# Conv columns scaled once by the squared row factor, the heads' forms on one engine, and a staging tile with a second use

## The chip, the cores and the metric

The kernel runs on one core of one Trainium2 chip. The metric is the device time of one launch in microseconds (us); less is better. A core has a matrix engine (TensorE, PE in the profile, with its weight loads as PEld), three engines for elementwise work (VectorE or DVE, ScalarE or ACT, GpSimd or POOL), a queue that issues transfers (SP) and 16 DMA engines. The engines run on their own and wait for each other by semaphores. Operands lie in on-chip memory (SBUF); TensorE writes its sums to PSUM banks.

## The reference

One layer of a hybrid encoder is applied to 512 prompt frames and 64 sample frames (576 together) of width 2048, in fp32. What matters here is the middle of it:

```
hn = rmsnorm(x, g_norm1);  proj = hn @ w_in
q, k, v, gb, gc, hc = split(proj)          # 8 heads x 128, and three times 1024 conv channels
u = gc * hc
conv = conv_w[0]*u[t-2] + conv_w[1]*u[t-1] + conv_w[2]*u[t]
o_conv = gb * conv
mix = concat(rmsnorm(o_attn, g_attn_out), rmsnorm(o_conv, g_conv_out))
x = x + mix @ w_out                         # then a gated feed-forward block, untouched by the change
```

`rmsnorm(y, g) = y * rsqrt(mean(y*y) + EPS) * g`, with EPS = 1e-6. The first norm multiplies each frame (row) by a factor R = rsqrt(mean(x*x) + EPS). It is not applied to x ahead of the product but to what comes out of it: q, k and v per head, and the three conv columns gb, gc and hc. The last two rows of u are an output (the conv state), so u itself has to come out with its true scale.

## The kernel before

**Layout.** Frames lie along the free dimension, channels on the 128 partitions. The 576 frames are worked in two halves of 288 (`HALVES`). Every fp32 operand of a product is held as two parts, a high part rounded to the matrix format and the low rest: `split` makes the high part with a ScalarE copy (L230) and the low part with a VectorE subtraction (L231), or on another engine where one is given. A product of two such operands is three matmuls of 128x288.

**Stages.** First the eight heads, each with three column chunks of w_in (`head`, `project`). Then the conv channels: the first two of eight groups in the plain way (`conv_group`, `STD = 2`), the other six in nine *units* of two groups' columns each. A unit is computed by a scheme with 7 half-size products for 8 (`conv_run`), whose operands are sums of quarters of the weights and of the frames. Units are of kind u (gc and hc of one group, six of them) and b (gb of two groups, three of them). Products are numbered here as they stand in `corder`: product 0 is (unit 0, part 1), then (0,2), (1,1), (1,2), (0,7), (0,6), (0,5), (0,3), (0,4), (1,6), (1,7), (1,5), (2,1), (1,3), (1,4). Then eight units "o" multiply the heads' outputs by w_out in the same way, and `out_proj` multiplies the conv outputs. The feed-forward block follows.

**The row factor in the conv columns.** `R1` holds R, the same on all partitions, 128x576. In the plain groups the gate gc is multiplied by R1 twice on its way out of PSUM (L960, L961), since gc and hc each want one factor, hc is multiplied by the gate straight from PSUM (`put_u`, L933 and L935), and gb is multiplied by R1 (L975) before the taps (L950, L952). In the units `done` multiplies each of the four quarters by R1 (L1112), after the addition of a partial sum where there is one (L1110). `put_mix` makes the two parts of the result times g_conv_out, stores them to DRAM and adds their squares to `acc_c` (squares on ScalarE, the addition on POOL at L538). Late in the o units, `group_scale` splits those sums, adds them over the channels with a product against ones (`channel_sums`) and turns them into the factor `R_c` (`rsqrt_mean`).

**The heads' forms.** Once the heads are done, `head_forms` normalises their outputs and makes, for each of four pairs of heads, the seven *forms* (three quarters and four differences of quarters) that the o units need. Each form is split into the staging tile `bt["stage"]` (named hf in the profile; eight slots of two parts, used in turn) and stored to DRAM (L580). The sums of squares of the heads, `acc_a`, are split ahead of that into two tiles of the pool tag hl (two buffers, which `put_mix` uses as well). The four differences per pair are made on POOL (L586), the low parts of forms 5 and 6 on POOL too, all else on VectorE.

**What sets the order.** The work beside the products is written as generators that a small scheduler (`Pipeline`) advances by one tick per step of a product, so it is spread in the program between the matmuls. TensorE's order is the program's. ScalarE, VectorE, POOL and SP are ordered by a planner that simulates the program with modelled durations, except in stretches set by hand; from the last half of the second conv group to product 8, ScalarE and VectorE go in program order (`start_mode`). `conv_prepare` makes the operands of a product (`whl`) some products ahead, `begin` sets which at the start, and `call_columns` loads the next weight columns as soon as a half of `raw_a`, or `raw_c`, is free. All form stores, weight loads and the loads of frame sums (xs) are issued on SP, in order.

Of the kernel before, what the change touches and what calls it, by code (L numbers as in the profile page):

```python
# [13 lines left out]
ALU = mybir.AluOpType  # L14
PSUM = bass.MemoryType.PSUM

P = 128
TP = 512
TS = 64
T = TP + TS  # L20
HALF = T // 2
HALVES = ((0, HALF), (HALF, T))
# [9 lines left out]
EPS = 1e-6  # L32
NEG = -1.0e30
QB = TP // P
NP = KD // 2
# [59 lines left out]
def tile_hybrid_stream_step(  # L95
# [6 lines left out]
    nc = tc.nc  # L102
# [20 lines left out]
    NB = T // 32  # L123
    eps_r, gk_t, quad = small[:, :NB], small[:, NB : NB + 32], small[:, NB + 32 : NB + 36]
# [39 lines left out]
    def weight_raw(i):  # L164
        src, nk, ncol = specs[i]
        raw = raw_tile["A"][:, i % 2, : nk * ncol]
        return raw, raw.rearrange("p (k c) -> p k c", k=nk), src
# [61 lines left out]
    def split(hi, lo, src, lo_eng=None):  # L229
        nc.scalar.copy(out=hi, in_=src)  # L230
        (lo_eng or nc.vector).tensor_tensor(out=lo, in0=src, in1=hi.bitcast(F32), op=ALU.subtract)  # L231

    def parts(name):
        t = tmp.tile([P, 2, HALF], F32R, tag="hl", name=name)
        return t[:, 0], t[:, 1]
# [72 lines left out]
    def col(name, i=0):  # L308
        return vec[:, rows[name] + i : rows[name] + i + 1]
# [18 lines left out]
    R1 = rpool.tile([P, T], F32, tag="R", name="R1", bufs=2)  # L328
# [63 lines left out]
    with tc.manual_schedule(engines={mybir.EngineType.Activation, mybir.EngineType.DVE, mybir.EngineType.SP}):  # L392
        raw, raw3, src = weight_raw(0)
# [25 lines left out]
        for kt in range(KD + LAG):  # L419
# [21 lines left out]
            if kt == 16:  # L441
                nc.vector.tensor_tensor(out=lo1[:, :1024], in0=raws[1][:, :1024], in1=hi1[:, :1024].bitcast(F32),  # L442
                                        op=ALU.subtract)
# [7 lines left out]
        while squares:  # L451
# [13 lines left out]
                            in1=quad.unsqueeze(1).to_broadcast([P, 5, 4]), op=ALU.mult)  # L465
# [17 lines left out]

    hpool.release()

    def rsqrt_mean(dst, src, n, width, ms=None, t=None):
        if ms is None:
            ms = tmp.tile([P, HALF], F32, tag="ms", name="ms", bufs=1)[:, :width]
            t = tmp.tile([P, HALF], F32, tag="t", name="t", bufs=1)[:, :width]
        y = tmp.tile([P, HALF], F32, tag="y", name="y")[:, :width]  # L490
        nc.vector.tensor_scalar(out=ms, in0=src, scalar1=1.0 / n, scalar2=EPS, op0=ALU.mult, op1=ALU.add)
        nc.scalar.activation(out=y, in_=ms, func=AF.Ln)
        nc.scalar.activation(out=y, in_=y, func=AF.Exp, scale=-0.5)
        nc.vector.tensor_tensor(out=t, in0=y, in1=y, op=ALU.mult)
        nc.vector.scalar_tensor_tensor(out=t, in0=t, scalar=-0.5, in1=ms, op0=ALU.mult, op1=ALU.mult)
        nc.vector.scalar_tensor_tensor(out=dst, in0=t, scalar=1.5, in1=y, op0=ALU.add, op1=ALU.mult)
# [58 lines left out]
    def head_forms():  # L555

        turn = [0]
        two = [parts("sqg") for _ in HALVES]  # L560
        for (sh, sl), (a, b) in zip(two, HALVES):
            split(sh, sl, acc_a[:, a:b])
        yield 6
        for (sh, sl), (a, b) in zip(two, HALVES):
            rsqrt_mean(acc_a[:, a:b], channel_sums(sh, sl, a, b, "ssg"), 8 * P, HALF)
            yield 4
        for k in range(NH // 2):
            pair = o_half[k // 2][:, 2 * (k % 2) : 2 * (k % 2) + 2, :]
            four = pair.rearrange("p k (i t) -> p (k i) t", i=2)
            b11, b12, b21, b22 = (four[:, q, :] for q in range(4))  # L570
            for r in range(2):
                nc.vector.scalar_tensor_tensor(out=pair[:, r], in0=pair[:, r], scalar=col("ga", 2 * k + r), in1=acc_a,
                                               op0=ALU.mult, op1=ALU.mult)
            yield 2

            def put(f, src, lo_eng):
                t = bt["stage"][:, turn[0] % NP]
                turn[0] += 1
                split(t[:, 0], t[:, 1], src, lo_eng)
                nc.sync.dma_start(out=form_dram[f - 1, k].rearrange("f p t -> p f t"), in_=t.bitcast(F32))  # L580

            for f, src in ((1, b11), (2, b21), (3, b22)):
                put(f, src, nc.vector)
                yield 2
            for f, out, a, b in ((5, b11, b12, b11), (7, b12, b12, b22), (6, b22, b22, b11), (4, b21, b21, b22)):
                nc.gpsimd.tensor_tensor(out=out, in0=a, in1=b, op=ALU.subtract)  # L586
                yield 1
                put(f, out, nc.gpsimd if f in (5, 6) else nc.vector)
                yield 2
            if k == 1:  # L590
                bt["raw"] = apool.tile([P, 2048], F32, tag="oa", name="raw_c")
                assert cwanted[0] == (1, 0)
                call_columns([2])

    def group_scale(acc, dst, rows_of):

        four = cpool.tile([P, 2, 2, HALF], F32R, tag="uc", name="sqg")
        for i, (a, b) in enumerate(HALVES):
            sh, sl = four[:, i, 0], four[:, i, 1]
            split(sh, sl, acc[:, a:b])  # L600
            yield rows_of
            ss = channel_sums(sh, sl, a, b, "ssg")
            ms, t = (tmp.tile([P, HALF], F32, tag=tag, name=tag + "g") for tag in ("r", "sq"))
            rsqrt_mean(dst[:, a:b], ss, 8 * P, HALF, ms, t)
            yield rows_of

    acc_a = rpool.tile([P, T], F32, tag="R", name="acc_a", bufs=2)
# [289 lines left out]
    bt = {}  # L897
# [45 lines left out]
            nc.vector.scalar_tensor_tensor(out=c, in0=u[:, r : UW - 2 + r], scalar=col("cw", r * NG + g), in1=c,  # L943
                                           op0=ALU.mult, op1=ALU.add)

    def put_o(g, i, t):

        a, b = HALVES[i]
        c, e = taps(g), min(b, TP)
        nc.vector.tensor_tensor(out=t[:, : e - a], in0=t[:, : e - a], in1=c[:, a:e], op=ALU.mult)  # L950
        if b > TP:
            nc.vector.tensor_tensor(out=t[:, e - a :], in0=t[:, e - a :], in1=c[:, TP + 2 :], op=ALU.mult)  # L952
        put_mix(g, i, t, col("gc", g), bt["acc"][:, a:b], g == 0)

    def conv_group(g):
        gates = []

        def evac_gc(ps, a, b):
            t = tmp.tile([P, HALF], F32, tag="sq", name="gcr")
            nc.vector.tensor_tensor(out=t, in0=ps, in1=R1[:, a:b], op=ALU.mult)  # L960
            nc.vector.tensor_tensor(out=t, in0=t, in1=R1[:, a:b], op=ALU.mult)  # L961
            gates.append(t)

        project(evac_gc)
        begin_u(g)
        project(lambda ps, a, b: put_u(a, b, ps, gates[a // HALF]),
                then=(lambda: call_columns(range(2))) if g == STD - 1 else None)

        def evac_gb(ps, a, b):
            if not bt:  # L970
                open_b()
            if a == 0:
                end_u(g)
            t = tmp.tile([P, HALF], F32, tag="y", name="gbr")
            nc.vector.tensor_tensor(out=t, in0=ps, in1=R1[:, a:b], op=ALU.mult)  # L975
            put_o(g, a // HALF, t)

        if g == STD - 1:
            for p_ in (1, 2):
                conv_prepare(0, p_)  # L980

            last_half = []
            project(lambda ps, a, b: last_half.append((ps, a, b)) if a else evac_gb(ps, a, b))
            start_mode.enter_context(tc.manual_schedule(engines={mybir.EngineType.Activation,
                                                                 mybir.EngineType.DVE}))
            conv_prepare(1, 1)
            evac_gb(*last_half[0])
            return
        project(evac_gb)


# [98 lines left out]
    def conv_run(n, p_):  # L1090
# [7 lines left out]
        def done(c, i, ps, part=None):  # L1098
            a, b = HALVES[i]
            tag = {(0, 0): "sq", (1, 1): "y"}.get((c, i), "r") if kind == "u" else "y"  # L1100
            if kind == "o":
                x = x2(2 * g + c)[:, a:b]
                if part is None:
                    nc.scalar.copy(out=x, in_=ps)
                else:
                    nc.vector.tensor_tensor(out=x, in0=ps, in1=part, op=ALU.add)
                return
            t = st[c, i] = tmp.tile([P, HALF], F32, tag=tag, name="cv")
            if part is not None:
                nc.vector.tensor_tensor(out=t, in0=ps, in1=part, op=ALU.add)  # L1110
                ps = t
            nc.vector.tensor_tensor(out=t, in0=ps, in1=R1[:, a:b], op=ALU.mult)  # L1112
            if kind == "b":
                put_o(g + c, i, t)
            elif (1 - c, i) in st:
                if i:
                    begin_u(g)
                put_u(a, b, st[0, i], st[1, i])
# [76 lines left out]
    def x2(kt):  # L1195
        return x2t[kt // 2][:, kt % 2, :]

    start_mode = ExitStack()
    for g in range(STD):
        conv_group(g)  # L1200
# [26 lines left out]
    for k_, (n, p_) in enumerate(corder):  # L1227
# [7 lines left out]
        if n == NCU - 1 and p_ in (6, 7, 4):  # L1235
            q = {6: 1, 7: 2, 4: 3}[p_]
            t = bt["pool"].tile([P, NH, 2, HALF], F32R, tag=f"t{q}", name=f"forms{q}")
# [430 lines left out]
    for d, v in visits.items():  # L1668
        n = next(a for a, b in zip(v, v[1:]) if a >= NGU + 10 and b >= a + 4)
# [246 lines left out]
```

## Time and profile before

| | us |
|---|---|
| median of 3 runs | 2354.87 (2354.53 to 2357.86) |
| profiled execution, its own time | 2357.63 |
| its span, first to last instruction | 2355.9 |
| TensorE busy | 2335.7 |
| VectorE busy | 1890.2 |
| ScalarE busy | 1138.5 |
| POOL busy | 298.6 |

The profile is of one execution. TensorE's granted clock was 1.00 throughout the stages around the change. Names in the profile are the program's: psy, psx and psw are PSUM banks of the units, pj those of the plain projections, whl the operands of a product, cv the quarters of a unit, gcr and gbr the columns gc and gb. A timeline row gives start, length, engine, line, operation, out<-in, shape and count; in brackets stands the idle time before it and what ended that. A wait row gives total, times and the longest.

### The profile page before, as it was taken

How to read it: one execution, taken by the hardware profiler on the slowest of the kernel's cores; microseconds unless marked ns; L12 is line 12 of the kernel's file. 1: busy time of each engine (PE TensorE's matmuls, PEld its weight loads, DVE VectorE, ACT ScalarE, POOL GpSimd, SP SyncE). 2: the span in 40 equal slices, each digit the busy share in tenths (PEclk: the TensorE clock that was granted, in tenths of full speed). 3: DMA queues.
4: the chain of work that ended last, by engine and by line, in shares of the span. 5: the costliest groups of instructions: out<-in, count | busy, mean ns of one | idle time of the engine just before them, and what ended most of it. 6: DMA issues, size and time to landing. Idle time of an engine off the chain costs nothing.

```text
span 2355.9 us, 43774 instructions
## 1 busy us (share of the span) xinstructions
PE 2335.7 (99%) x17573; PEld 2326.5 (99%) x17573; DVE 1890.2 (80%) x2822; ACT 1138.5 (48%) x1989; POOL 298.6 (13%) x401
## 2 busy tenths in 40 slices
PE   9999999999999999999999999999999999999999
PEld 8999999989999999999999999999999999999999
DVE  7766665788887899888888888888888778887896
ACT  6655565434444555444444444444444444444444
POOL 1111111422121230000000000000000002431221
PEclk9999999999999999999999999999999999999999
DMA  8665563773468555344344444444444936885553
GB/s 267 164 167 145 135 163 108 247 232 114 124 235 225 177 170 162 123 154 152 123 153 137 139 153 140 135 153 128 148 153 131 355 122 201 226 238 189 199 133 101
DMA packets 581795, 395.74 MB, mean 168 GB/s; under 512 B 90718, under 2 KB 570712, under 8 KB 581592
## 3 DMA queue, kind: packets, MB, share of 16 engines
q1 hardware_dynamic: 572168, 376.28, 51.2%
q0 software_dynamic: 8624, 16.22, 3.3%
q8 instruction: 137, 2.24, 0.4%
q14 instruction: 66, 0.54, 0.1%
q10 hardware_dynamic: 800, 0.46, 0.1%
HBM read 301.46 MB, written 91.44 MB: 167 GB/s over the span
## 4 chain that ended last, share of the span: by engine, by line
PE 86%; DVE 8%; DMA 3%; ACT 2%; issue 1%; POOL 0%; SPq 0%; DVEq 0%; ACTq 0%; POOLq 0%
PE psy L1582 34%; PE psw L1582 17%; PE pj L221 13%; PE psx L1582 9%; PE psy L1086 5%; PE psw L1086 3%; PE psx L1086 1%; DMA raw_a<-in_w_out_dram 1%; DVE wlo L178 1%; DMA raw_a<-in_w_in_dram 1%; DVE whl L231 1%; DVE whl L1058 1%; PE z L723 1%; PE pjo L221 1%; PE po L794 1%
## 5 line engine op out<-in xcount | busy, mean ns | idle before, releaser
L1582 PE MATMUL psy<-h_s,whl 128*128 128x288 f32 x2787 | 411.1, 294 | 0.0
L221 PE MATMUL pj<-x,whi 128*128 128x288 f32 x1856 | 388.6, 298 | 0.3 <-DVE x L375 0.3
L1582 PEld LDWEIGHTS psy<-h_s,whl 128*128 128x128 f32 x2787 | 383.2, 188 | 0.1
L231 DVE TENSOR_TENSOR whl<-raw_a,whl 128x1024 fp32r<-128x1024 f32 (+4 forms) x296 | 322.4, 1090 | 56.7 <-ACT whl L230 55.4
L1582 PE MATMUL psw<-t,whl 128*128 128x288 f32 x2400 | 347.2, 294 | 0.0
L1582 PEld LDWEIGHTS psw<-t,whl 128*128 128x128 f32 x2400 | 327.8, 188 | 0.0
L230 ACT CAST whl<-raw_a 128x1024 fp32r<-128x1024 f32 (+4 forms) x296 | 267.9, 906 | 113.3 <-issue 35.6
L221 PEld LDWEIGHTS pj<-x,whi 128*128 128x128 f32 x1856 | 303.9, 189 | 1.1 <-DVE x L375 0.7
L221 PE MATMUL pj<-x,wlo 128*128 128x288 f32 x928 | 274.5, 296 | 0.1
L231 DVE TENSOR_TENSOR whl<-raw_b,whl 128x1024 fp32r<-128x1024 f32 (+5 forms) x190 | 198.1, 1042 | 65.9 <-ACT whl L230 65.0
L230 ACT CAST whl<-raw_b 128x1024 fp32r<-128x1024 f32 (+5 forms) x190 | 165.0, 871 | 169.8 <-issue 72.8
L1592 ACT COPY part<-psy 128x288 f32<-128x288 f32 x242 | 96.5, 399 | 273.9 <-PE psy L1582 271.2
L1582 PE MATMUL psy<-b22m,whl 128*128 128x288 f32 x1212 | 182.7, 294 | 0.8 <-ACT part L1592 0.8
L1582 PE MATMUL psy<-t2t,whl 128*128 128x288 f32 x1212 | 183.0, 294 | 0.0
L221 PEld LDWEIGHTS pj<-x,wlo 128*128 128x128 f32 x928 | 174.8, 188 | 0.7 <-DVE wlo L442 0.3
L1582 PE MATMUL psx<-h_s,whl 128*128 128x288 f32 x1185 | 173.5, 294 | 0.0
L1582 PEld LDWEIGHTS psy<-b22m,whl 128*128 128x128 f32 x1212 | 168.0, 188 | 1.0 <-ACT part L1592 1.0
L1582 PEld LDWEIGHTS psy<-t2t,whl 128*128 128x128 f32 x1212 | 168.3, 188 | 0.2 <-DVE whl L231 0.2
L1582 PEld LDWEIGHTS psx<-h_s,whl 128*128 128x128 f32 x1185 | 162.6, 188 | 0.0
L1361 POOL DMA_DIRECT2D hid_dram<-form x3 | 2.2, 749 | 947.2 <-DVE form L231 947.2
L230 ACT CAST whl<-s 128x1024 fp32r<-128x1024 f32 (+5 forms) x81 | 72.2, 892 | 99.4 <-PE psw L1582 99.2
L1582 PE MATMUL psy<-t,whl 128*128 128x288 f32 x576 | 106.6, 295 | 0.0
(474 smaller groups left out, 4306.6 us busy)
## 6 DMA issues: line engine op xcount, KB each, us to landing
hid_dram<-form SPq DMA_DIRECT2D x147, 288.0 KB, 2.3
raw_a<-in_w_in_dram SPq DMA_DIRECT2D x41, 1024.0 KB, 6.0
raw_a<-in_w_gate_dram SPq DMA_DIRECT2D x22, 1024.0 KB, 5.5
raw_a<-in_w_up_dram SPq DMA_DIRECT2D x22, 1024.0 KB, 5.9
raw_b<-in_w_gate_dram SPq DMA_DIRECT2D x22, 1024.0 KB, 6.6
raw_b<-in_w_up_dram SPq DMA_DIRECT2D x22, 1024.0 KB, 6.9
h_s<-hid_dram SPq DMA_DIRECT2D x10, 2016.0 KB, 12.3
raw_a<-in_w_out_dram SPq DMA_DIRECT2D x16, 1024.0 KB, 5.7
```

Source lines behind the costliest of these rows:

```text
L178: lo_eng.tensor_tensor(out=lo[:, a:b], in0=raw[:, a:b], in1=hi[:, a:b].bitcast(F32), op=ALU.subtract)
L221: mm(ps, w_[:, k, csl], x_, start=(k == 0 and n == 0), stop=(k == nk - 1 and n == 2))
L230: nc.scalar.copy(out=hi, in_=src)
L231: (lo_eng or nc.vector).tensor_tensor(out=lo, in0=src, in1=hi.bitcast(F32), op=ALU.subtract)
L723: mm(zb[i], a_[:, kk], b_[:, q0:TP], start=(n == 0), stop=False, skip_group_check=True)
L794: mm(po[:, i * P : 512], a_[:, i, :], b_[:, : 512 - i * P], stop=(i == 0 and n == 2), **kw)
L1058: tt(out=whl[:, 1], in0=src, in1=whl[:, 0].bitcast(F32), op=ALU.subtract)
L1086: mm(ps, whl[:, w_, j, :], x_, start=(start and j == 0 and q == 0), stop=(j == m - 1 and q == 2), skip_group_check=True)
L1361: q.dma_start(out=hid_dram[fp][2 * n - 2 : 2 * n].rearrange("f p t -> p f t"), in_=t.bitcast(F32))
L1582: mm(ps, whl[:, w_, j, :], x_, start=(start and j == 0 and q == 0), stop=(j == len(xs_) - 1 and q == 2), skip_group_check=True)
L1592: nc.scalar.copy(out=t, in_=st["y"])
```

## The change

Three things are changed.

1. *Row factor.* R1 is squared once, in place, after the heads. The gate gc gets this squared factor in one multiplication; in the units only the quarters of the gate (c == 0) are multiplied. gb gets none: in the plain groups and in the b units it goes to the taps as it comes out of PSUM or of the addition. The conv output is then smaller by R per frame than before. `group_scale` makes up for it: where EPS was added, EPS/R**2 is added now. `eps_r` already holds that per frame in another layout; a ScalarE copy spreads it over 32 columns each and a VectorE transpose brings it to R_c's layout, in R_c itself.
2. *Forms.* The four differences per pair and the low parts of forms 5 and 6 move from POOL to VectorE.
3. *Parts of the squares.* The two halves of `acc_a` are split into the last two slots of the staging tile, where two buffers of tag hl were used.

```diff
-    def rsqrt_mean(dst, src, n, width, ms=None, t=None):
+    def rsqrt_mean(dst, src, n, width, ms=None, t=None, eps=None):
...
-        nc.vector.tensor_scalar(out=ms, in0=src, scalar1=1.0 / n, scalar2=EPS, op0=ALU.mult, op1=ALU.add)
+        if eps is None:
+            nc.vector.tensor_scalar(out=ms, in0=src, scalar1=1.0 / n, scalar2=EPS, op0=ALU.mult, op1=ALU.add)
+        else:
+            nc.vector.scalar_tensor_tensor(out=ms, in0=src, scalar=1.0 / n, in1=eps, op0=ALU.mult, op1=ALU.add)
...
-        two = [parts("sqg") for _ in HALVES]
+        two = [(bt["stage"][:, NP - 2 + i, 0], bt["stage"][:, NP - 2 + i, 1]) for i in range(2)]
...
-                nc.gpsimd.tensor_tensor(out=out, in0=a, in1=b, op=ALU.subtract)
+                nc.vector.tensor_tensor(out=out, in0=a, in1=b, op=ALU.subtract)
                 yield 1
-                put(f, out, nc.gpsimd if f in (5, 6) else nc.vector)
+                put(f, out, nc.vector)
...
         four = cpool.tile([P, 2, 2, HALF], F32R, tag="uc", name="sqg")
+        nc.scalar.copy(out=dst.rearrange("p (b c) -> p b c", c=32), in_=eps_r.unsqueeze(2).to_broadcast([P, NB, 32]))
+        nc.vector.transpose(out=dst, in_=dst)
...
-            rsqrt_mean(dst[:, a:b], ss, 8 * P, HALF, ms, t)
+            rsqrt_mean(dst[:, a:b], ss, 8 * P, HALF, ms, t, eps=dst[:, a:b])
...
-    def put_o(g, i, t):
+    def put_o(g, i, src, t):
...
-        nc.vector.tensor_tensor(out=t[:, : e - a], in0=t[:, : e - a], in1=c[:, a:e], op=ALU.mult)
+        nc.vector.tensor_tensor(out=t[:, : e - a], in0=src[:, : e - a], in1=c[:, a:e], op=ALU.mult)
         if b > TP:
-            nc.vector.tensor_tensor(out=t[:, e - a :], in0=t[:, e - a :], in1=c[:, TP + 2 :], op=ALU.mult)
+            nc.vector.tensor_tensor(out=t[:, e - a :], in0=src[:, e - a :], in1=c[:, TP + 2 :], op=ALU.mult)
...
             nc.vector.tensor_tensor(out=t, in0=ps, in1=R1[:, a:b], op=ALU.mult)
-            nc.vector.tensor_tensor(out=t, in0=t, in1=R1[:, a:b], op=ALU.mult)
             gates.append(t)
...
             t = tmp.tile([P, HALF], F32, tag="y", name="gbr")
-            nc.vector.tensor_tensor(out=t, in0=ps, in1=R1[:, a:b], op=ALU.mult)
-            put_o(g, a // HALF, t)
+            put_o(g, a // HALF, ps, t)
...
-            nc.vector.tensor_tensor(out=t, in0=ps, in1=R1[:, a:b], op=ALU.mult)
             if kind == "b":
-                put_o(g + c, i, t)
-            elif (1 - c, i) in st:
+                put_o(g + c, i, ps, t)
+                return
+            if c == 0:
+                nc.vector.tensor_tensor(out=t, in0=ps, in1=R1[:, a:b], op=ALU.mult)
+            else:
+                st[c, i] = ps
+            if (1 - c, i) in st:
...
+    nc.vector.tensor_tensor(out=R1, in0=R1, in1=R1, op=ALU.mult)
     start_mode = ExitStack()
```

## The prediction

> **What bounds the kernel now.** I read the page first, then busy time by stretch, then TensorE's timeline in the one stretch where it idles, then the chain of waits through that stretch, and last the groups and waits of the engines that the change touches.
>
> ```profile
> span 2355.9 us, 43774 instructions
> ...
> PE 2335.7 (99%) x17573; PEld 2326.5 (99%) x17573; DVE 1890.2 (80%) x2822; ACT 1138.5 (48%) x1989; POOL 298.6 (13%) x401
> ```
>
> TensorE bounds the kernel: 20 of 2355.9 us are idle, and the change gives it no instruction more or less. All that the change touches lies between 390 and 780 us, and most of TensorE's idle time in that stretch stands in some 40 us of it. Its timeline there (start, length, then in brackets the idle time before it and the releaser):
>
> ```profile
> 475.40 3.33 PE L1086 MATMUL psy<-x,whl 128*128 128x288 f32 x24
> ...
> 482.38 0.40 PE L1086 MATMUL psy<-x,whl 128*128 128x288 f32 x1 [0.47 <-ACT whl L1055]
> 483.64 3.31 PE L1086 MATMUL psy<-x,whl 128*128 128x288 f32 x23 [0.86 <-DVE whl L1058]
> 488.43 3.44 PE L1086 MATMUL psx<-x,whl 128*128 128x288 f32 x24 [1.48 <-DVE cv L1110]
> ...
> 492.43 3.31 PE L1086 MATMUL psw<-xs_t,whl 128*128 128x288 f32 x23 [0.43 <-DVE whl L1058]
> ...
> 509.55 3.31 PE L1086 MATMUL psy<-xs_t,whl 128*128 128x288 f32 x23 [0.86 <-DVE whl L1058]
> ...
> 517.21 9.70 PE L1086 MATMUL psy<-x,whl 128*128 128x288 f32 x71 [1.04 <-DVE whl L1058]
> 526.74 3.33 PE L1086 MATMUL psw<-xs_t,whl 128*128 128x288 f32 x24
> ```
>
> The six waits add up to 5.14 us, but a modelled matmul end hides part of each. Counted by starts: 475.40 is product 0 of the conv units, 526.74 is product 14. The pace of an undisturbed product is 3.17 us (chain, below), so 14 should take 44.4 us; they took 51.34. **6.9 us are lost here**, and that is what can be won. Why, from the chain of waits:
>
> ```profile
> 472.31 5.33 DMA form_dram<-hf
> ...
> 482.37 1.22 DVE whl L1058
> ...
> 488.77 1.15 DVE raw_a L1044
> ...
> 496.00 8.59 DMA raw_a<-in_w_in_dram
> ...
> 508.27 1.23 DVE whl L1058
> ...
> 515.93 1.23 DVE whl L1058
> ...
> 530.07 3.17 PE psx L1086 x24
> ```
>
> The first units' operands (whl) stand on ScalarE and VectorE behind the heads' forms (tile hf), which end at 482.4. All that follows is late with them: the operand of product 2 at 482.37, the sums of unit 0 at 488.77, the load into the half of raw_a that those sums free at 496.00, and so product 9 at 509.55 and product 11 at 517.21.
>
> **The change part by part.** The forms, 442.6 to 482.4, by groups (count, busy us, mean ns, idle before):
>
> ```profile
> L231 DVE TENSOR_TENSOR hf<-o_ob,hf 128x288 fp32r<-128x288 f32 x10 | 8.5, 869 | 2.9 <-ACT hf L230 2.9
> L231 DVE TENSOR_TENSOR hf<-o_oa,hf 128x288 fp32r<-128x288 f32 x10 | 8.1, 824 | 0.0
> L572 DVE SCALAR_TENSOR_TENSOR o_ob<-o_ob,vec,acc_a 128x576 f32<-128x576 f32 x4 | 4.9, 1220 | 0.0
> L572 DVE SCALAR_TENSOR_TENSOR o_oa<-o_oa,vec,acc_a 128x576 f32<-128x576 f32 x4 | 3.7, 951 | 0.0
> ...
> L961 DVE TENSOR_TENSOR gcr<-gcr,R 128x288 f32<-128x288 f32 x2 | 2.1, 1056 | 0.0
> ...
> L960 DVE TENSOR_TENSOR gcr<-pj,R 128x288 f32<-128x288 f32 x2 | 0.9, 448 | 0.0
> ```
>
> ```profile
> L586 POOL TENSOR_TENSOR o_ob<-o_ob 128x288 f32<-128x288 f32 x8 | 8.5, 1066 | 4.0 <-DVE hf L231 3.8
> L586 POOL TENSOR_TENSOR o_oa<-o_oa 128x288 f32<-128x288 f32 x8 | 8.1, 1009 | 4.7 <-DVE hf L231 4.4
> L231 POOL TENSOR_TENSOR hf<-o_oa,hf 128x288 fp32r<-128x288 f32 x4 | 4.4, 1096 | 0.0
> L231 POOL TENSOR_TENSOR hf<-o_ob,hf 128x288 fp32r<-128x288 f32 x4 | 3.4, 862 | 0.0
> ```
>
> ```profile
> 450.91 0.81 DVE L572 SCALAR_TENSOR_TENSOR o_oa<-o_oa,vec,acc_a 128x576 f32<-128x576 f32 x1
> ...
> 478.21 4.17 DVE L231 TENSOR_TENSOR hf<-o_ob,hf 128x288 fp32r<-128x288 f32 x2 [1.07 <-ACT hf L230]
> ```
>
> ```profile
> 478.58 0.82 POOL L586 TENSOR_TENSOR o_ob<-o_ob 128x288 f32<-128x288 f32 x1
> ...
> 480.88 0.80 POOL L231 TENSOR_TENSOR hf<-o_ob,hf 128x288 fp32r<-128x288 f32 x1
> ```
>
> ```profile
> ACT hf L230 <- POOL o_ob L586: 8.6, 5, 3.5
> ACT hf L230 <- DMA form_dram<-hf: 5.7, 3, 5.0
> ACT hf L230 <- POOL o_oa L586: 5.2, 7, 1.5
> ```
>
> ```profile
> 442.60:482.40 39.80, 39.33 (x299) 39.09 (x297) 36.06 (x46) 17.60 (x36) 28.20 (x31) 1.00 0.94 308
> ...
> 450.00:460.00 10.00, 10.00 (x78) 10.00 (x77) 10.00 (x13) 5.78 (x12) 7.05 (x7) 1.00 0.75 246
> ```
>
> Forms on VectorE: 16 subtractions and 8 low parts come from POOL. A 128x288 operation costs VectorE 0.45 us where nothing disturbs it (L960, from PSUM); 24 are 10.8 us. Against that stands what POOL costs VectorE. An operation with both inputs in SBUF takes 1.06 (L961) beside POOL, and the pair at 478.21 lasted 4.17 us while POOL ran four instructions back to back. Taken back to 0.45 us, the 20 low parts give 16.6 - 9.0 = 7.6; the eight 128x576 scalings at 0.81 (the one at 450.91) give 8.6 - 6.5 = 2.1. With L961 gone (2.1): 36.06 + 10.8 - 7.6 - 2.1 - 2.1 = 35.1 us. VectorE is then through at 477.7 without idle time, or at 481.4 if the 3.7 us that it idles now stay. I take 478 to 479: ScalarE's 13.8 us of waiting for POOL go, each form becoming ready behind a 0.45 us subtraction where POOL took 1.0. Late next is the transfer: 5.7 us of ScalarE's waits are for a staging slot to be written out. The stretch moved 308 GB/s; the slice at 450 moved 246 at share 0.75, so there is room for faster forms early. SP's queue issues the same 28 writes, the loads of unit operands and the xs loads in the same order.
>
> ```profile
> L1112 DVE TENSOR_TENSOR cv<-cv,R 128x288 f32<-128x288 f32 x28 | 13.8, 496 | 0.5
> ```
>
> ```profile
> L668 DVE STREAM_TRANSPOSE kf<-Ek x8: 778/780/781, 58.0 to 385.2; 128x576 f32<-128x576 f32 x8
> ```
>
> ```profile
> 418.34 0.67 ACT L230 CAST sph<-sp 128x576 fp32r<-128x576 f32 x1 [3.88 <-PE po L794]
> ```
>
> Factors: of the 36 multiplications at L1112 (four in each of nine units; the row shows 28), 24 go: four in each of three b units, two in each of six u units. 24 x 0.49 = 12 us of VectorE over 200 us; none is on the path except one between products 9 and 11 (0.4 us). The four at L961 and four at L975 go, 3.6 us undisturbed. R1 squared is one 128x576 operation of about 0.8 us between the last head's value columns and the first gate; hidden, since three banks take projections. With 0.45 us less behind each gate, VectorE is ahead again after two.
>
> L950 and L952 now read PSUM, so a bank is held until the taps are ready; in the traced order the taps precede them already: nothing. The rows show PSUM (L960, 448) no dearer than SBUF (L1112, 496, some beside POOL). [...]
>
> group_scale: one ScalarE copy (0.67) and one transpose (0.78) more, ready to run as soon as the R buffer is free, long before the output projection wants R_c; without that cover 1.5 us. Squares in the stage: no instruction moves off an engine; the second half no longer waits for a buffer of tag hl, but its sums stand at a fixed place in TensorE's order: between 0 and 0.4 us earlier, taken as nothing. The stage is touched earlier than now, in memory that the heads' tiles leave, but the xs loads into the same pool are issued before that. Forms use the two slots again only at turns 6 and 7.
>
> **The sum.** Product 2 is due at 475.40 + 2 x 3.17 = 481.74. Its operand needs 1.2 us behind the forms: about 480, in time, and products 3 and 4 follow. The sums at 488.77 can start when product 1 is out of PSUM, about 482.6: 6.1 us earlier. The load then ends no later than 498.5, and the operand of product 9, now done at 509.5, at 503.4; due is 475.40 + 9 x 3.17 = 503.9. Product 11 is due at 510.3; its operand trails that of product 9 by 7.7 us now, 7.3 without one multiplication: 502.2 + 7.3 + 1.2 = 510.7. That leaves some 0.4, and I leave 0.3 for places unforeseen: 6.9 - 0.7 = **6.2 us won**. The profiled span goes from 2355.9 to 2349.7. That execution took 2357.63, 1.73 beside its span and 2.76 above the median of 2354.87; the median goes to 2348.7.
>
> **The rivals.** Transfers set the pace (0.22): the forms are produced faster, then wait for slots as they do at 472.31. Then only the 3.3 us go that the pair at 478.21 lost to POOL; what follows is 3.3 us earlier: 2351.6. The 5.7 us of slot waits speak for it, the slice at 450 against it. That the forms' end doesn't reach TensorE, 2354.9, shares those 0.22.
>
> VectorE becomes the bound (0.16, slower): if its long operations are not POOL's doing but come from transfers into SBUF, the 9.7 us of relief don't come. Then 36.06 + 10.8 - 2.1 = 44.8 us, the forms end at 487.4, and TensorE waits 5.0 longer: 2359.9. It decides where less than 5.0 of the 9.7 us come (487.4 - 482.4), or less than 8.7 if VectorE idles as now. Against it: L960, in the same stretch, took 448. [...]
>
> One more wait of TensorE, from 700 to 870 us (total, times, longest), enters the range:
>
> ```profile
> PE psy L1086 <- ACT part L1095: 1.3, 2, 0.7
> ```
>
> **How the numbers follow.** Forecast 0.62, transfers 0.22, VectorE 0.16. A measurement of this kernel tells about 0.2%, 4.7 us, from no change. The forecast is beyond it, transfers within, VectorE beyond it on the other side: chances 0.62, 0.22, 0.16. Below, the range takes the whole 6.9 and the 1.3 us that TensorE waits for w_out's units between 700 and 870 (the row above), should those go too: 2354.87 - 8.2 = 2346.7. Above it ends at 2353.5, short of no effect, which leaves out VectorE's case and a part of transfers.
>
> **What would show it.** Right: in the stretch to 482 no POOL tensor operations, low parts at 0.45 us, the last form before 479, product 14 some 44.4 to 45 us behind product 0. Wrong: slot waits of ScalarE above 5.7 us, a wait of TensorE before 475 on pj, forms ending after 482, or new waits between 530 and 780 that give the time back.

## The result and the profile after

The changed kernel takes 2351.92 us (median of 16 runs, 2349.75 to 2354.34). The kernel before, run on the same occasion, takes 2356.98 (16 runs, 2354.53 to 2359.06). The ratio is 0.9979 with a 95% interval of 0.9972 to 0.9986: 5.1 us faster, where 6.2 were forecast. The profiled execution took 2351.68, 1.68 beside its span. The median of the kernel before stood at 2354.87 when there were 3 runs of it and at 2356.98 with 16, so 2.1 of the 3.2 us between the forecast of 2348.7 and the measured median lie in the starting point, and 1.1 in the gain.

The page of the changed kernel, its span and busy times:

```profile
span 2350.0 us, 43733 instructions
...
PE 2334.7 (99%) x17573; PEld 2326.4 (99%) x17573; DVE 1873.3 (80%) x2816; ACT 1139.4 (48%) x1990; POOL 273.7 (12%) x377
```

Busy time by stretch, the changed kernel (columns: from:to and length, then busy us of TensorE, weight load, VectorE, ScalarE and POOL with instruction counts, granted clock, DMA share, GB/s):

```profile
442.60:478.00 35.40, 35.40 (x270) 35.40 (x269) 33.59 (x68) 18.20 (x37) 4.93 (x7) 1.00 1.07 352
...
475.00:530.00 55.00, 54.14 (x408) 53.67 (x407) 45.87 (x59) 23.88 (x31) 9.39 (x12) 1.00 0.66 212
```

The same second stretch of the kernel before:

```profile
475.00:530.00 55.00, 49.86 (x366) 48.43 (x365) 45.08 (x55) 23.46 (x34) 12.12 (x14) 1.00 0.69 224
```

In the 55 us from 475 TensorE was idle for 5.1 us before and is idle for 0.9 now. The forms, in the first row, now end with VectorE 33.6 us busy in 35.4, and POOL's 28.2 us have become 4.9. TensorE's timeline after, in the stretch where the prediction looked for the gain:

```profile
476.03 3.33 PE L1089 MATMUL psy<-x,whl 128*128 128x288 f32 x24
...
504.59 0.29 PE L1089 MATMUL psy<-xs_t,whl 128*128 128x288 f32 x1
505.06 3.31 PE L1089 MATMUL psy<-xs_t,whl 128*128 128x288 f32 x23 [0.18 <-DVE whl L1061]
...
512.37 9.68 PE L1089 MATMUL psy<-x,whl 128*128 128x288 f32 x71 [0.68 <-DVE whl L1061]
521.88 3.33 PE L1089 MATMUL psw<-xs_t,whl 128*128 128x288 f32 x24
```

The waits ahead of products 2, 3 and 4 are gone; products 9 and 11 still wait. Product 0 to product 14 takes 521.88 - 476.03 = 45.85 us, against 51.34 before. From here on *lost* means this time less the prediction's 44.4: 6.9 before, 1.45 after, so 5.5 us are won in this stretch. Product 0 itself started 0.6 later than before, at 476.03, and the span is 5.9 shorter (2355.9 to 2350.0): 5.5 less 0.6, and 1.0 more behind product 14.

All operations on the forms' tile on VectorE, after (count, shortest/median/longest in ns, first and last start):

```profile
L231 DVE TENSOR_TENSOR hf<-o_oa,hf x14: 446/451/458, 444.8 to 459.5; 128x288 fp32r<-128x288 f32 x14
...
L231 DVE TENSOR_TENSOR hf<-o_ob,hf x14: 436/450/459, 459.8 to 477.2; 128x288 fp32r<-128x288 f32 x14
```

Every one of the 28 low parts takes 0.45 us, the value that the prediction took, and none is stretched. ScalarE's waits from 442 to 480, after (total, times, longest):

```profile
ACT hf L230 <- DMA form_dram<-hf: 5.7, 5, 2.4
```

The waits for a staging slot (the releaser form_dram<-hf, a form's store) are still 5.7 us in all, yet the forms end at 477.6 where they ended at 482.4.

What stands behind the two waits that remain is in the chain of waits, after:

```profile
495.23 3.19 PE psx L1089 x24
...
498.44 0.41 ACT part L1146
...
498.93 0.80 POOL part L1148
...
499.76 0.46 DVE cv L1113
500.21 1.15 DVE raw_a L1047
...
503.78 1.23 DVE whl L1061
...
511.10 1.23 DVE whl L1061
...
512.37 9.68 PE psy L1089 x71
```

Product 6 (the psx at 495.23) ends at 498.4. Its result goes through a ScalarE copy, a POOL addition and a VectorE addition, and only then do the sums start from which the operands of products 9 and 11 are made. In this execution the forms are not in the chain any more; in two further executions of the same kernel they are, by way of a load (whole_again and whole_third, below).

### The profile page after: what moved, and what is told of

Same layout as the page of the kernel before. It is cut to its first block, busy times and chain, and to the rows that moved or that the text cites. A ratio compares the mean times of both kernels' runs of the same rounds, so it can differ in the third digit from the quotient of the medians.

```text
span 2350.0 us, 43733 instructions
## 1 busy us (share of the span) xinstructions
PE 2334.7 (99%) x17573; PEld 2326.4 (99%) x17573; DVE 1873.3 (80%) x2816; ACT 1139.4 (48%) x1990; POOL 273.7 (12%) x377
## 4 chain that ended last, share of the span: by engine, by line
PE 94%; DVE 2%; DMA 2%; ACT 1%; issue 0%; SPq 0%; POOL 0%; ACTq 0%; DVEq 0%
PE psy L1590 34%; PE psw L1590 17%; PE pj L221 15%; PE psx L1590 9%; PE psy L1089 6%; PE pjo L221 4%; PE psw L1089 3%; PE psx L1089 2%; DMA raw_a<-in_w_out_dram 1%; PE pjz L221 1%; PE po L799 1%; PE z L728 1%; DVE whl L231 0%; PE os L829 0%; PE zs L754 0%
## 5 line engine op out<-in xcount | busy, mean ns | idle before, releaser
L221 PE MATMUL pj<-x,whi 128*128 128x288 f32 x1856 | 388.7, 298 | 0.3 <-DVE x L375 0.3
L230 ACT CAST whl<-raw_a 128x1024 fp32r<-128x1024 f32 (+4 forms) x296 | 267.8, 906 | 113.4 <-issue 35.4
L221 PEld LDWEIGHTS pj<-x,whi 128*128 128x128 f32 x1856 | 304.0, 189 | 1.0 <-DVE x L375 0.6
L221 PE MATMUL pj<-x,wlo 128*128 128x288 f32 x928 | 274.5, 296 | 0.1
L221 PEld LDWEIGHTS pj<-x,wlo 128*128 128x128 f32 x928 | 174.8, 188 | 0.7 <-DVE wlo L442 0.3
```

The lines of the kernel that those rows point to most:

```text
L221: mm(ps, w_[:, k, csl], x_, start=(k == 0 and n == 0), stop=(k == nk - 1 and n == 2))
```

## The experiments

All are ratios to the kernel before on the same chip, with 95% intervals. "Lost" is taken from the starts of products 0 and 14 in each run's profiled execution. pool_reads has 6 runs, the others 10 or 11.

| run | ratio | median us | lost us |
|---|---|---|---|
| forms_alone | 0.9985 (0.9977 to 0.9994) | 2352.76 | 2.3 |
| squares_alone | 0.9999 (0.9990 to 1.0007) | 2356.23 | 5.6 |
| factor_alone | 1.0009 (0.9999 to 1.0018) | 2358.64 | 2.9 |
| whole_again | 0.9983 (0.9974 to 0.9992) | 2351.77 | 2.2 |
| no_forms | 0.9991 (0.9982 to 0.9999) | 2354.27 | 4.3 |
| no_squares | 1.0004 (0.9995 to 1.0012) | 2357.81 | 1.45 |
| no_factor | 0.9983 (0.9975 to 0.9992) | 2352.84 | 2.3 |
| pool_reads | 1.0031 (1.0019 to 1.0042) | 2363.82 | 7.7 |
| pool_writes | 0.9978 (0.9969 to 0.9987) | 2351.60 | 1.4 |
| shorter_chain | 0.9976 (0.9967 to 0.9985) | 2350.89 | 0.55 |
| whole_third | 0.9981 (0.9972 to 0.9990) | 2351.29 | 2.5 |

The first four share a chip, so do no_forms, no_squares and the two POOL runs, and so do the other three. The whole change lost 1.45, 2.2 and 2.5 us in its three profiled executions, so a difference of one microsecond in this column is within what one execution differs from the next.

### Each part alone, and the whole again

forms_alone: the kernel before, with the forms' part alone.

```diff
-                nc.gpsimd.tensor_tensor(out=out, in0=a, in1=b, op=ALU.subtract)
+                nc.vector.tensor_tensor(out=out, in0=a, in1=b, op=ALU.subtract)
...
-                put(f, out, nc.gpsimd if f in (5, 6) else nc.vector)
+                put(f, out, nc.vector)
```

> Only the forms' part of the change. My theory (what POOL held up, the ends of the forms and of all behind them, is the gain): nearly all of the whole change's 5.5 us between products 0 and 14 comes, 4.5 to 5.5, since only the one multiplication between products 9 and 11 (0.4 us) and L961 (2.1 us in the forms' stretch, which has room) are missing; the time falls by 4 to 5 us, ratio 0.9979 to 0.9984. Rival (the factors' 16 us less on VectorE carry the gain): at most 1 us, ratio 0.9996 to 1.0. Rival (VectorE becomes the bound, 10.8 us more on it): slower.

TensorE's timeline, forms_alone:

```profile
505.44 0.29 PE L1086 MATMUL psy<-xs_t,whl 128*128 128x288 f32 x1
506.40 3.33 PE L1086 MATMUL psy<-xs_t,whl 128*128 128x288 f32 x23 [0.68 <-DVE whl L1058]
...
514.08 9.66 PE L1086 MATMUL psy<-x,whl 128*128 128x288 f32 x71 [1.04 <-DVE whl L1058]
```

These are its only two waits between products 0 and 14: those of products 2, 3 and 4 are gone with the forms' part alone, and lost falls from 6.9 to 2.3. That is 4.6 us, inside the 4.5 to 5.5 expected; the ratio is just above the range. Product 11 waits 1.04 as it did before the change.

squares_alone: the kernel before, with the squares' parts in the staging tile.

```diff
-        two = [parts("sqg") for _ in HALVES]
+        two = [(bt["stage"][:, NP - 2 + i, 0], bt["stage"][:, NP - 2 + i, 1]) for i in range(2)]
```

> Only the squares' parts in the staging tile. My theory: TensorE takes the sums of squares at a fixed place of its order, so the forms start within 0.4 us of before; ratio 0.9998 to 1.0002. Rival (the wait for a buffer of tag hl delays the forms): the forms start some 2 us earlier and the time falls by 1 to 2 us, ratio 0.9992 to 0.9996.

No difference in time. The first form's high part is made at 443.5 as before, and products 2, 3 and 4 wait as before. By itself this part is worth nothing, as predicted.

factor_alone: the whole change, with the other two parts taken back.

```diff
-        two = [(bt["stage"][:, NP - 2 + i, 0], bt["stage"][:, NP - 2 + i, 1]) for i in range(2)]
+        two = [parts("sqg") for _ in HALVES]
...
-                nc.vector.tensor_tensor(out=out, in0=a, in1=b, op=ALU.subtract)
+                nc.gpsimd.tensor_tensor(out=out, in0=a, in1=b, op=ALU.subtract)
...
-                put(f, out, nc.vector)
+                put(f, out, nc.gpsimd if f in (5, 6) else nc.vector)
```

> Only the row factor's part; POOL makes the differences and two low parts as before. My theory: the forms still end at about 480 to 482, held by POOL and by the wait for slots; TensorE loses 6 to 7 us between products 0 and 14 as before, less up to 1; ratio 0.9995 to 1.0. Rival (the factors carry the gain): those products lose under 3 us, ratio 0.9980 to 0.9988.

Neither the theory (6 to 7 us lost) nor the rival (a better time) came out: the 2.9 us lost look like a gain, yet the time is not better than before. The reason lies ahead of product 0, which starts at 481.37. ScalarE's timeline, factor_alone:

```profile
431.16 0.43 ACT L230 CAST sqg<-acc_a 128x288 fp32r<-128x288 f32 x1
...
438.96 0.43 ACT L230 CAST sqg<-acc_a 128x288 fp32r<-128x288 f32 x1 [7.02 <-DMA mix_dram<-mx]
```

TensorE's timeline, factor_alone:

```profile
439.44 0.40 PE L503 MATMUL ssg<-sqg,oner 128*128 128x288 f32 x1 [3.49 <-ACT sqg L230]
```

The second half of the heads' squares waits 7.0 us for a buffer of tag hl that a conv result (mx) holds until its store has landed. The product against ones behind it stands at a fixed place in TensorE's order, so TensorE waits 3.5 us, which it did not before. In the kernel before, the same second half waited 2.0 us, for the first half's products, and TensorE not at all.

whole_again: the changed kernel once more, beside these three.

> The whole change beside its parts on one chip. My theory: 0.9976 to 0.9982, the sum of the parts within 1 us, since each part works on the same stretch and only the forms' part takes waits away. Rival (the parts need each other): the whole is faster than the sum of its parts by more than 1.5 us.

Products 9 and 11 wait 0.86 and 0.69, all others not at all. The theory that the gains of the parts add up failed, and the rival came out: 0.9985, 0.9999 and 1.0009 multiply to 0.9993, the whole has 0.9983, which is some 2.4 us faster. What the parts need of each other is shown by no_squares below.

### The whole change without one part

no_forms: the whole change, with the differences and the low parts of forms 5 and 6 back on POOL (the edit of forms_alone, reversed).

> The whole change without the forms' part (POOL makes them again). In the run of the factor alone the second half of the squares waited 7.0 us for a buffer of tag hl that a transfer was still reading, and TensorE 3.5 us for it; here the squares lie in the staging tile. My theory now: that wait is gone and the forms end 3 to 4 us behind product 0's start, as in the factor's run, where they ended 7 us behind it before; the products lose 2.5 to 4 us of 6.9; ratio 0.9982 to 0.9990. Rival (the factor's run lost fewer because TensorE was late there): the products lose 5.5 to 6.9, ratio 0.9993 to 1.0.

Operations on the forms' tile, no_forms:

```profile
L231 DVE TENSOR_TENSOR hf<-o_oa,hf x10: 446/992/1062, 443.7 to 460.3; 128x288 fp32r<-128x288 f32 x10
```

These low parts are back at a median of 0.99 us, products 2, 3 and 4 wait 0.64, 0.99 and 0.46, and lost is 4.3. The expectation was missed narrowly (2.5 to 4 lost; the forms end 5.6 us behind product 0's start, not 3 to 4), and its rival too (5.5 to 6.9). The gain is then 0.9 in a thousand; with the forms' part it is 1.7 to 2.1.

no_squares: the whole change, with two buffers of tag hl for the squares' parts.

```diff
-        two = [(bt["stage"][:, NP - 2 + i, 0], bt["stage"][:, NP - 2 + i, 1]) for i in range(2)]
+        two = [parts("sqg") for _ in HALVES]
```

> The whole change without the squares' part (their parts lie in two buffers of tag hl again). My theory now: with the multiplications gone the buffer that falls to the second half is the one whose transfer is under way; TensorE waits 3 to 4 us at the second sum of squares, product 0 starts 5 us later than in the whole change, and the time goes back to within 1 us of before: ratio 0.9996 to 1.0006. Rival (that wait came from POOL making the forms): no wait of TensorE there, ratio 0.9977 to 0.9984 as with the whole change.

The chain of waits, no_squares:

```profile
430.04 0.53 DVE mx L554
...
430.89 6.87 DMA mix_dram<-mx
...
437.86 0.44 ACT sqg L230
...
438.83 0.40 PE ssg L504
439.23 5.80 PE pj L221 x32
```

TensorE's timeline, no_squares:

```profile
438.34 0.40 PE L503 MATMUL ssg<-sqg,oner 128*128 128x288 f32 x1 [3.21 <-ACT sqg L230]
```

The wait of factor_alone is back: the store takes 6.9 us to land, TensorE waits 3.2 us, and product 0 starts at 480.31. From there on the stretch is as good as in the whole change (1.45 lost), but some 5 us at its head are given away again. Busy time by stretch, no_squares:

```profile
440.00:442.00 2.00, 2.00 (x10) 2.00 (x9) 1.34 (x5) 0.87 (x2) 0.00 (x0) 0.50 1.08 392
```

The granted clock in this stretch is 0.50, where it was 1.00 ahead of the wait and is 1.00 again from 444: the 32 matmuls at L221 take 5.80 us in the chain, where at the undisturbed pace of 24 in 3.17 they would take 4.2. The wait of 3.2 us so costs some 1.6 us more than itself.

So the squares' part is worth nothing next to the forms' part alone, but the factor's part cannot do without it. Which hl buffer the second half gets is decided in the program's plan; that the factor's shorter path for gb (one multiplication less ahead of mx) changes the turn is inferred from the two traces and was not tried by itself.

no_factor: the kernel before, with the edits of forms_alone and squares_alone together.

> The forms' and the squares' part without the row factor's. My theory (the forms' part takes the waits away; the squares' part only stands against a wait that the factor's part brings): as with the forms alone, 2 to 2.5 us lost between products 0 and 14, no wait of TensorE at the sums of squares, ratio 0.9978 to 0.9988. Rival (the factor's part gives a gain of its own of 2 us or more on top of the forms): 0.9985 to 0.9992, 3 us or more lost.

TensorE's timeline and the chain of waits, no_factor:

```profile
505.13 3.31 PE L1086 MATMUL psy<-xs_t,whl 128*128 128x288 f32 x23 [0.67 <-DVE whl L1058]
...
512.78 9.69 PE L1086 MATMUL psy<-x,whl 128*128 128x288 f32 x71 [1.04 <-DVE whl L1058]
```

```profile
499.33 0.47 DVE cv L1110
...
499.82 0.46 DVE cv L1112
500.28 1.15 DVE raw_a L1044
```

Product 11 waits 1.03 or 1.04 in all four kernels without the factor's part (before, forms_alone, squares_alone and this one) and 0.65 to 0.70 in all with it, shorter_chain aside. Product 9 waits 0.67 here and 0.68 in forms_alone, but 0.18 in the five executions with the factor's part in which its sums follow product 6 as they do here (after, factor_alone, no_forms, no_squares and pool_writes). The chain shows why: without the factor's part a multiplication by R1 (L1112) stands between product 6's quarter and the sums. So of the 24 multiplications taken from VectorE the waits show two that lay on the path, 0.5 us ahead of product 9 and 0.35 ahead of product 11. In time the two kernels can't be told apart: 0.9983 here and 0.9981 for whole_third on the same chip.

### POOL beside VectorE: reads against writes

pool_reads: the whole change, with four POOL additions of constant tiles behind each difference (64 in all; the results go to columns that nothing reads).

```diff
-        bt["acc"] = acon.tile([P, T], F32, tag="ac", name="acc_c")
+        both_c = acon.tile([P, 6 * P], F32, tag="ac", name="acc_c")
+        bt["acc"], bt["idle"] = both_c[:, :T], both_c[:, T:]
...
+                for _ in range(4):
+                    nc.gpsimd.tensor_tensor(out=bt["idle"][:, :P], in0=ident, in1=vec, op=ALU.add)
```

> The whole change, and beside it POOL adds two constant tiles into a spare one 64 times (128x128) while VectorE makes the forms; nothing waits for these. My theory (POOL's reads of SBUF hold up VectorE's operations with two SBUF inputs): the forms' low parts on VectorE grow from 0.45 us to 0.6 or more in the mean, those with an input in PSUM stay at 0.45, the forms end 2 us later or more against product 0. Rival (transfers into SBUF made VectorE's operations long): 0.45 us as without.

pool_writes: the same, but POOL only writes, eight fills of 192 columns behind each difference.

```diff
-                for _ in range(4):
-                    nc.gpsimd.tensor_tensor(out=bt["idle"][:, :P], in0=ident, in1=vec, op=ALU.add)
+                for _ in range(8):
+                    nc.gpsimd.memset(bt["idle"], 0.0)
```

> As pool_reads, but POOL only writes: 128 times a fill of 192 columns of the spare tile. My theory (only POOL's reads stand in VectorE's way): low parts of 0.45 us, the forms end where they do in the whole change, the time is that of the whole change, ratio 0.9976 to 0.9984. Rival (any work of POOL on SBUF holds VectorE up): the low parts grow as with reads.

Operations on the forms' tile, pool_reads:

```profile
L231 DVE TENSOR_TENSOR hf<-o_oa,hf x14: 443/712/715, 451.6 to 471.7; 128x288 fp32r<-128x288 f32 x14
...
L231 DVE TENSOR_TENSOR hf<-o_ob,hf x14: 439/448/1416, 472.4 to 490.0; 128x288 fp32r<-128x288 f32 x14
```

The same, pool_writes:

```profile
L231 DVE TENSOR_TENSOR hf<-o_oa,hf x14: 449/454/460, 444.6 to 458.8; 128x288 fp32r<-128x288 f32 x14
```

VectorE's timeline, pool_reads, in the middle of 41 POOL additions that follow one another without a break for 29.9 us from 438.45:

```profile
462.50 0.71 DVE L589 TENSOR_TENSOR o_oa<-o_oa 128x288 f32<-128x288 f32 x1
463.14 0.45 DVE L968 TENSOR_TENSOR gcr<-pj,R 128x288 f32<-128x288 f32 x1
463.51 0.44 DVE L589 TENSOR_TENSOR o_oa<-o_oa 128x288 f32<-128x288 f32 x1
```

POOL's timeline, pool_writes:

```profile
444.69 26.21 POOL L591 MEMSET acc_c<- 128x192 f32 x83
```

Beside POOL instructions that read, the low part takes 0.71 us where it takes 0.45 without them; the operation of the same size with one input from PSUM (pj) takes 0.45 right beside it. POOL's additions end at 474.7, and the low parts on o_ob, most of them made after that, are at a median of 0.45 in the same execution. Not every operation is held: the one right behind the operation from PSUM has both inputs in SBUF and took 0.44. The forms end 8.4 us behind product 0's start, where after the change it is 1.6. Beside POOL instructions that only write, at least as busily (83 in 26.2 us without a break), the low part stays at 0.454 and the time is that of the whole change (0.9978). So VectorE's long operations beside POOL are POOL's doing, not that of the transfers, which run in all these kernels (low parts of 0.71 us at a DMA share of 0.27 in pool_reads, 448 to 455, and of 0.45 at 1.07 after the change, 442.6 to 478); that the kernel before is the same case rests on its low parts, which are long with POOL's tensor operations beside them (0.82 to 0.87 in the mean) and 0.45 without.

The time of pool_reads, 1.0031, is not the price of this alone. Its POOL additions were also planned ahead of the addition of the last squares to acc_a, so TensorE waited 3.0 us at the second sum of squares, ran at a granted clock of 0.50 until 445, and product 0 started at 482.06.

### The chain that is left

shorter_chain: the whole change, where the last quarter of unit 0 is summed earlier. Its two partial sums are added on VectorE as soon as product 5 allows, and product 6's result is added straight from PSUM, in place of the ScalarE copy, POOL addition and VectorE addition one after the other. (The part numbers in the code are those of the scheme: part 6 is product 5, part 5 is product 6.)

```diff
         elif p_ == 6:
             conv_multiply(st["y"], n, 6, False)
             st["u2"] = kept("r" if n == NCU + 1 else "t")
+            if n == 0:
+                st[1, 1] = tmp.tile([P, HALF], F32, tag="y", name="cv")
+                nc.vector.tensor_tensor(out=st[1, 1], in0=st["w"], in1=st["u2"], op=ALU.add)
...
-            u4 = tmp.tile([P, HALF], F32, tag="ms", name="part", bufs=1)
-            nc.gpsimd.tensor_tensor(out=u4, in0=st["p5"], in1=st["u2"], op=ALU.add)
-            done(1, 1, st["w"], u4)
+            nc.vector.tensor_tensor(out=st[1, 1], in0=x, in1=st[1, 1], op=ALU.add)
```

> The whole change, and in unit 0 the last quarter is put together otherwise: its two partial sums are added on VectorE before product 6 is through, and the bank of product 6 is added straight after it (before: a ScalarE copy, a POOL addition and a VectorE addition in a row, 498.4 to 500.2). My theory (what is left of the loss hangs on product 6, no longer on the forms): the sums for product 9 start 1.2 us earlier, product 9 waits under 0.1 us and product 11 under 0.3 us, 0.6 us or less lost between products 0 and 14 where the whole change loses 1.4 to 2.2; time 1 us below the whole change, ratio 0.9972 to 0.9980. Rival (the load into raw_a or the end of the forms still sets it): product 9 waits as before.

The chain of waits, shorter_chain:

```profile
494.40 3.19 PE psx L1089 x24
...
497.61 0.41 ACT part L1149
...
498.04 0.46 DVE cv L1150
498.50 1.14 DVE raw_a L1047
...
502.06 1.23 DVE whl L1061
```

From product 6's end to the start of the sums it is 0.9 us now (497.6 to 498.5) where it was 1.8 (498.4 to 500.2). Product 9 doesn't wait any more, product 11 waits 0.24, and 0.55 us are lost, as expected; against product 0's start the sums come 0.9 us earlier than after the change, for 1.2 expected. That the load did not hold them is in part chance: it was issued at 490.00 and was there by 498.4, and with the 9.05 us that it took in whole_third it would have been later than product 6. The median, 2350.89, is the lowest of all kernels here; whole_third, on the same chip, has 2351.29, and the two intervals overlap widely, so that it is faster than the whole change is shown by the waits and not by the time. The wait for w_out's units between 700 and 870, 0.8 us after, was 2.0 here.

whole_third: the changed kernel once more, beside no_factor and shorter_chain.

> The whole change on the same chip as the two others, for comparison: 1.4 to 2.2 us lost between products 0 and 14, ratio 0.9974 to 0.9984.

The chain of waits, whole_third:

```profile
491.81 9.05 DMA raw_a<-in_w_in_dram
...
500.88 1.24 DVE raw_a L1047
```

In this execution the same sums wait for the load and not for product 6: issued at 491.81, it took 9.05 us, the sums stood 0.99 us for it, and product 9 waited 0.86. The loss of 2.5 is above the 1.4 to 2.2 expected. whole_again has the same (issued at 491.08, 8.74 us, the sums stood 0.69, product 9 waited 0.86). In both the forms end 2.6 us behind product 0's start, where it is 1.6 in the profile after, and ScalarE's waits for a staging slot are 9.3 and 6.8 us, not 5.7. So in two of three executions of the changed kernel it is still the forms' end that sets product 9, through the sums of unit 0 and the load; that the slot waits make the forms later in these two is inferred, no run changes them alone.

## Why the prediction was right

The time fell into the range and on the forecast's side; 5.1 us were won for 6.2. The interval of the ratio allows 3.3 to 6.6 us, so the time by itself hardly tells the forecast from the rival of the transfers (3.3 us won); the stretch does, with 5.5.

**What bounds the stretch.** Right. The forms' lateness carried the waits of products 2, 3 and 4: they go with the forms' part alone (forms_alone), and most of them come back without it (no_forms: 2.1 us of 3.2).

**VectorE's relief.** Right in kind and nearly in size. The low parts are at 0.45 us, VectorE is busy for 33.6 us to the end of the forms (35.1 were summed), and the last form ends at 477.6, just ahead of the 478 to 479 taken. One difference is still held up: it lasts over the issue of a store on POOL (from 473.89) and the one POOL addition that is left there (474.64 to 475.46). VectorE's timeline, after:

```profile
473.99 1.79 DVE L589 TENSOR_TENSOR o_ob<-o_ob 128x288 f32<-128x288 f32 x1
```

**The rivals.** Transfers as the pace fell: the slot waits did stay at 5.7 us, as that rival needed, but the forms end 4.8 us earlier all the same. A part of it is true in the other two executions, with 9.3 and 6.8 us of slot waits: above 5.7, a sign of being wrong by the prediction's own list, and about 1 us more is lost there. VectorE as the bound fell with the two POOL runs: the long operations are POOL's doing, as the forecast had it, and the low parts are long beside its reads (0.71 us) and not beside its fills (0.454).

**The step that was mis-sized.** "The sums at 488.77 can start when product 1 is out of PSUM, about 482.6: 6.1 us earlier." They start at 483.85. VectorE's timeline, after:

```profile
478.02 1.22 DVE L1061 TENSOR_TENSOR whl<-raw_c,whl 128x1024 fp32r<-128x1024 f32 x1 [0.39 <-ACT whl L1058]
...
481.85 1.23 DVE L1061 TENSOR_TENSOR whl<-raw_c,whl 128x1024 fp32r<-128x1024 f32 x1 [1.05 <-ACT whl L1058]
482.99 0.45 DVE L1113 TENSOR_TENSOR cv<-psx,part 128x288 f32<-128x288 f32 x1
483.48 0.46 DVE L1119 TENSOR_TENSOR cv<-cv,R 128x288 f32<-128x288 f32 x1
483.85 1.22 DVE L1047 TENSOR_TENSOR raw_a<-raw_a 128x1024 f32<-128x1024 f32 x1
```

VectorE goes in program order here, and between the forms and the sums stand two operands, the columns of the second conv group and two steps of a quarter, with 2.0 us in which VectorE waits for ScalarE. That makes 6.2 us from the forms' end to the sums (477.6 to 483.85), much as before (6.4, 482.4 to 488.8), and 6.2 in whole_again and whole_third too. So the sums are earlier by as much as the forms, 4.9 us against 4.8, and not by 6.1. Of the 1.2 us between, 0.6 are only that product 0 started later in this execution. Counted from product 1's end at the undisturbed pace, the sums start 1.5 us behind it here and 2.5 in whole_again and whole_third, where the prediction had 0.9. The rest follows: the load behind the sums is issued at 491.14 in place of 496.00, and with the 8.6 us that it took before would land at about 499.7, not by 498.5. There the chain from product 6 takes over, which the prediction did not look at: it ends at 500.2. The operand of product 9 is then ready at 505.0, 29.0 behind product 0, where 503.4 (28.0) was forecast. The 7.3 us from there to the operand of product 11 came out exactly (505.01 to 512.33). This one microsecond makes the 1.45 us lost in place of 0.7.

**Factors.** Right for the one multiplication that was named, 0.4 us forecast, 0.35 measured. The prediction's "none is on the path except one" missed another: that of product 6's quarter, which in the kernel before ended 0.2 us ahead of the load and so was hidden. With the load early it is worth 0.5 us ahead of product 9 (no_factor). The rest of VectorE's 12 us less over 200 us is there and shows in no wait: from 530 to 700 it is busy 136.67 us where it was 147.53. The taps that read PSUM (pj) cost no more than from SBUF: 0.38 us for 128x224 and 0.21 for 128x64 after (from 479.16), where they took 0.39 and 0.22 before (from 483.99). L955 with 128x288 took 417 ns among the forms, and the low parts from SBUF 450.

**group_scale.** Hidden, as taken: the copy ran at 468.65 and the transpose at 471.36, 0.77 us among the forms.

**Squares in the stage.** "Taken as nothing" was right for this part by itself (0.9999), but the step failed beside the factor's part. There it is what keeps the second half from waiting for a store: without it TensorE waits 3.2 us, runs at half the clock for some 3 us more, and the whole gain is gone (no_squares, 1.0004). The forecast stands in spite of this step by luck: the three parts came together, and the prediction did not see that two of them need each other.

**The range's low end.** The waits for w_out's units went from 1.3 to 0.8 us after, but they were 0.6 and 1.1 in the two other executions of the changed kernel, 1.3 in no_factor and 2.0 in shorter_chain; no gain of the change is seen in them.

## What to carry to other kernels

Count what is lost from the starts of the products against their undisturbed pace, and after each repair look for the next chain with the same end: here the load and the sum of product 6 ended within a microsecond of each other once the forms were early. Where VectorE goes in program order, work that is waited for comes earlier by as much as what stands ahead of it in that order, not by as much as its data: here the sums came 4.9 us earlier behind forms that ended 4.8 earlier, where 6.1 were forecast. A buffer that an outgoing transfer held was a wait of about that transfer's length here (ScalarE waited 6.7 us for a store of 6.9 in no_squares, and 7.0 for one of 7.1 in factor_alone), so take a part that frees such a buffer together with the part that makes it needed, and test parts in pairs and not only alone.

## What the runs showed of the hardware

- TensorE's granted clock fell to 0.50 after a wait of 3.2 us (no_squares, 440 to 443; the same after 3.5 us in factor_alone, 441 to 443, and after 3.0 us in pool_reads, 440 to 445) and came back to 1.00 some 4 to 6 us after the wait's end; after the waits of up to 1.48 us in the kernel before it stayed at 1.00 (478 to 496). In no_squares product 0 started 4.3 to 5.3 us later than in the three executions of the whole change.
- VectorE's low parts, 128x288 with two SBUF inputs, took 0.71 us in the median beside a dense row of POOL additions of 128x128 and 0.45 without it (pool_reads), 0.26 us more each. That is no bound: in the kernel before one low part lasted 3.80 us, most of the 4.17 of the pair at 478.21, until a row of five POOL instructions of 128x288 that began at 477.81 was over at 481.68. What makes the two rows differ so much was not tried.
